# A two-layer hybrid decoder in split float32: 512-column feature blocks taken two K tiles at a time, bias rows written by GpSimd copies, and a layer norm in another order

## The chip, the cores and the metric

The kernel runs on one NeuronCore of a Trainium2 chip. The metric is the device time of one execution in microseconds (us); times before and after are medians of several runs. Beside them stands the profile of one execution, taken by the hardware profiler. Engines are named as in the profile: PE is TensorE (PEld are its weight loads), DVE is VectorE, ACT is ScalarE, POOL is GpSimd, and SP is SyncE, which issues most of the DMAs.

## The reference

Two decoder layers on 256 tokens of width 1024, all in float32. Each layer projects the stream into three head groups (retention, block-sparse attention with a relative bias, a gated convolution), joins them by an output projection, adds and normalizes; then a gated MLP of width 2816 with a causal convolution of width 3 adds and normalizes again.

```python
def reference(x, w_in, conv_w, w_out, ln1_g, ln1_b, w_up, ffn_conv_w, w_down, ln2_g, ln2_b, rel_bias):
    for l in range(DEPTH):
        mix = hybrid_mixer(x, w_in[l], conv_w[l], w_out[l], rel_bias)
        x = layer_norm(DN_ALPHA * x + mix, ln1_g[l], ln1_b[l])
        f = conv_ffn(x, w_up[l], ffn_conv_w[l], w_down[l])
        x = layer_norm(DN_ALPHA * x + f, ln2_g[l], ln2_b[l])
    return x

def conv_ffn(h, w_up, ffn_conv_w, w_down):
    u = h @ w_up
    a, b = u[..., :D_FF], u[..., D_FF:]
    a = causal_dwconv(a, ffn_conv_w)
    return (jax.nn.gelu(a.astype(F32), approximate=False) * b.astype(F32)).astype(h.dtype) @ w_down
```

In the attention, `s_own = einsum(q, k) * scale + rel_bias[t5_bucket(q_pos - k_pos)]`, with masked positions at minus infinity. With 256 tokens there is one block, so the bias of a head depends on the distance 0 to 255 alone, through 32 buckets.

## The kernel before, in words

Every float32 operand is split into a high part of reduced precision and a low rest (`split`: ACT casts, DVE subtracts), and each product is made of three: high by high, low by high, high by low. Tokens are two tiles of 128 (`NT`), the width is eight K tiles of 128 (`KD`). Weights come in units of 512 KB: SP loads a unit into `raw` (5 buffers), ACT and DVE split it into `whi` and `wlo` (6 buffers), five units ahead of PE (`LOOKAHEAD`). A scheduler sets the order of the instructions on each engine from the program, so that an edit in one place can move rows in another.

PE passes through these stages in each layer: the value projections (lines 231 to 233, `mm3`), twelve feature blocks for attention and retention (lines 318 to 320 and 407 to 409), attention and retention woven with more feature blocks, the output projection, the first norm, the MLP, the second norm. The stages that the change touches are these:

- **Wide blocks** (`wide_block`, lines 645 and 646): 30 blocks in each layer, for features 3 to 17 of the MLP. For each K tile one product of 512 columns multiplies `whi` by the high and low halves of `xx` side by side, and one of 256 columns adds `wlo` by the high half into the second half of the bank.
- **Bias rows** (`load_rows`, `load_bias`): in layer 0, after K tile 6 of the value projections, a product of the table `rel` (33 by 6) with the 0/1 matrix `bucket` (33 by 384) gives one row of 384 bias values for each head; DVE copies it from PSUM to `row`, POOL writes it to `scratch` in DRAM, and three POOL DMAs read it back into `bias`, one diagonal shift for each partition. DVE adds `bias` to the attention scores at line 456.
- **Layer norm** (`layer_norm`): for each token tile, DVE forms the sum and its statistics by halves of 512 columns, POOL raises the variance to the power of -1/2 (line 224), and DVE then subtracts and scales (line 259) and multiplies by `rstd` and adds (line 264), half by half. The halves are named h0 and h1 here. PE transposes each finished half (line 279, `turn`), ACT and DVE split the result into `xx`, and the next products read it. In the MLP's first products (`first_up`), tile 1 waits for this; four transposes of the gate values (line 609, `first_turn`) stand between.

Of the kernel before, what the change touches and what calls it, by code (L numbers as in the profile page):

```python
# [10 lines left out]
F32 = mybir.dt.float32  # L11
# [11 lines left out]
NH = 6  # L23
# [23 lines left out]
BIAS_AT = 6  # L47
# [5 lines left out]
def hybrid_decoder(ctx: ExitStack, tc: tile.TileContext, x, xw, wva, wvb, wf, wt, w_out, wg, w_up, w_down,  # L53
                   conv_w, ffn_w, ln1_g, ln1_b, ln2_g, ln2_b, rel_bias,
                   c_ident, c_rot, c_decay, c_bucket, out):
# [110 lines left out]
    rel = cp.tile([BUCKETS + 1, NH], F32, name="rel")  # L166
# [19 lines left out]
    def load_rows():  # L186

        pr = att()
        nc.tensor.matmul(pr[:NH, :HW], rel, bucket[:BUCKETS + 1, :], start=True, stop=True)
        nc.vector.tensor_copy(row[:NH, :], pr[:NH, :HW])  # L190
        nc.gpsimd.dma_start(scratch, row[:NH, :])
# [11 lines left out]
    bucket = ap.tile([P, HW], F32, name="bucket", tag="t384", bufs=6)  # L203
    row = ap.tile([P, HW], F32, name="row", tag="t384", bufs=6)
    nc.vector.memset(rel, MASKED)
    xr = x.rearrange("(t p) d -> p t d", p=P)
    spread = [lambda: load((rel[:BUCKETS, :], rel_bias), (bucket[:BUCKETS + 1, :], c_bucket)),
# [31 lines left out]
    def layer_norm(t, ps, xin, g, b, xout, store=None, after=None, between=None):  # L239
# [15 lines left out]
        done = None  # L255
        for h in range(2):
            s = slice(512 * h, 512 * h + 512)
            with behind(None if store else done):
                nc.vector.scalar_tensor_tensor(xout[:, t, s], xout[:, t, s], mv[:, 0:1], g[:, s],
                                               op0=ALU.subtract, op1=ALU.mult)  # L260
            n = 256 if store and h and t else 512
            for a in range(512 * h, 512 * h + 512, n):
                s = slice(a, a + n)
# [20 lines left out]
    for k in range(KD):  # L284
# [6 lines left out]
        if k == BIAS_AT:  # L291
            load_rows()
            for i in range(3):
                load_bias(i)
# [5 lines left out]
    for l in range(DEPTH):  # L300
# [337 lines left out]
        def wide_block(*name):  # L638
# [4 lines left out]
            for k in range(KD):  # L643
                c = slice(k * P, k * P + P)
                nc.tensor.matmul(ps, hi[:, c], xx[:, k].rearrange("p s t -> p (s t)"), start=k == 0, stop=False)  # L645
                nc.tensor.matmul(ps[:, T:], lo[:, c], xx[:, k, 0, :], start=False, stop=k == KD - 1)  # L646
# [77 lines left out]

def _constants():
# [9 lines left out]
    dist = 255 - np.arange(384)  # L735
    n = np.maximum(dist, 0)
    half = BUCKETS // 2
    large = half + (np.log(np.maximum(n, 1).astype(f) / f(half)) / f(math.log(MAX_DIST / half)) * f(half)).astype(np.int32)
    b = np.where(n < half, n, np.minimum(large, BUCKETS - 1))
    bucket = np.zeros((BUCKETS + 1, 384), f)  # L740
    for i in range(384):
        bucket[b[i] if dist[i] >= 0 else BUCKETS, i] = 1.0
# [54 lines left out]
```

## Time and profile before

| | before |
|---|---|
| median of 3 runs | 619.19 us (618.71 to 619.77) |
| the profiled execution | 619.32 us |
| its span | 617.5 us |
| granted TensorE clock | 0.996 |
| PE busy | 606.7 us, 98% |
| DVE busy | 456.1 us, 74% |
| ACT busy | 351.9 us, 57% |
| POOL busy | 15.4 us, 2% |

The span reaches from the first to the last instruction of the program; 1.8 us of the profiled execution lie around it. The duration that the profile gives to a product includes its way through the array, so that products overlap in the record. What a product costs in a row of them is read from start to start.

### The profile page before, as it was taken

How to read it: one execution, taken by the hardware profiler on the slowest of the kernel's cores; microseconds unless marked ns; L12 is line 12 of the kernel's file. 1: busy time of each engine (PE TensorE's matmuls, PEld its weight loads, DVE VectorE, ACT ScalarE, POOL GpSimd, SP SyncE). 2: the span in 40 equal slices, each digit the busy share in tenths (PEclk: the TensorE clock that was granted, in tenths of full speed). 3: DMA queues.
4: the chain of work that ended last, by engine and by line, in shares of the span. 5: the costliest groups of instructions: out<-in, count | busy, mean ns of one | idle time of the engine just before them, and what ended most of it. 6: DMA issues, size and time to landing. Idle time of an engine off the chain costs nothing.

```text
span 617.5 us, 10157 instructions
## 1 busy us (share of the span) xinstructions
PE 606.7 (98%) x3846; PEld 536.4 (87%) x3846; DVE 456.1 (74%) x834; ACT 351.9 (57%) x637; POOL 15.4 (2%) x18
## 2 busy tenths in 40 slices
PE   8999999999999999999999999999999999999994
PEld 6899998888888888899889999987888888888993
DVE  5478889787667676788765788878866767677846
ACT  6579847265555556566346795552665555656620
POOL 0100010000000000000000000101000000000001
PEclk9999999999999999999999999999999999999998
DMA  8988357465665665668428425672765666565401
GB/s 293 371 285 257 92 167 247 162 214 196 199 179 190 188 183 188 204 213 273 129 97 264 149 80 168 197 241 94 252 192 180 194 186 183 188 200 183 163 1 68
DMA packets 33676, 115.94 MB, mean 188 GB/s; under 512 B 3957, under 2 KB 4764, under 8 KB 33628
## 3 DMA queue, kind: packets, MB, share of 16 engines
q1 hardware_dynamic: 33356, 114.50, 57.6%
q0 software_dynamic: 272, 0.80, 0.4%
q8 instruction: 30, 0.49, 0.3%
q14 instruction: 18, 0.15, 0.1%
HBM read 114.22 MB, written 1.06 MB: 187 GB/s over the span
## 4 chain that ended last, share of the span: by engine, by line
PE 94%; DVE 3%; DMA 1%; POOL 1%; issue 0%; SPq 0%; ACT 0%; DVEq 0%; POOLq 0%
PE acc L645 18%; PE acc L646 9%; PE att L231 7%; PE att L232 7%; PE att L233 6%; PE acc L231 5%; PE acc L233 5%; PE acc L232 5%; PE acc L319 5%; PE acc L320 5%; PE acc L318 5%; PE acc L407 4%; PE acc L408 4%; PE acc L409 4%; PE att L346 1%; DVE x L264 1%
## 5 line engine op out<-in xcount | busy, mean ns | idle before, releaser
L83 DVE TENSOR_TENSOR wlo<-raw,whi 128x1024 fp32r<-128x1024 f32 (+3 forms) x207 | 228.5, 1115 | 80.7 <-ACT whi L82 80.2
L82 ACT CAST whi<-raw 128x1024 fp32r<-128x1024 f32 (+3 forms) x207 | 197.3, 963 | 99.0 <-PE acc L645 41.9
L645 PE MATMUL acc<-xx,whi 128*128 128x512 f32 x480 | 170.7, 398 | 0.0
L646 PE MATMUL acc<-xx,wlo 128*128 128x256 f32 x480 | 134.7, 281 | 0.0
L645 PEld LDWEIGHTS acc<-xx,whi 128*128 128x128 f32 x480 | 90.2, 188 | 22.0
L646 PEld LDWEIGHTS acc<-xx,wlo 128*128 128x128 f32 x480 | 90.6, 189 | 1.3
L319 PE MATMUL acc<-xx,whi 128*128 128x256 f32 x240 | 67.9, 283 | 0.0
L320 PE MATMUL acc<-xx,wlo 128*128 128x256 f32 x240 | 67.9, 283 | 0.0
L318 PE MATMUL acc<-xx,whi 128*128 128x256 f32 x240 | 67.9, 283 | 0.0
L407 PE MATMUL acc<-xx,whi 128*128 128x256 f32 x208 | 60.1, 289 | 0.0
L408 PE MATMUL acc<-xx,whi 128*128 128x256 f32 x208 | 58.8, 283 | 0.0
L409 PE MATMUL acc<-xx,wlo 128*128 128x256 f32 x208 | 58.8, 283 | 0.0
L232 PE MATMUL att<-whi,hl 128*128 128x512 f32 x144 | 56.5, 392 | 0.0
L233 PE MATMUL att<-wlo,hh 128*128 128x512 f32 x144 | 56.1, 389 | 0.0
L231 PE MATMUL att<-whi,hh 128*128 128x512 f32 x144 | 55.7, 393 | 0.0
L231 PE MATMUL acc<-whi,xx 128*128 128x512 f32 (+2 forms) x128 | 46.1, 363 | 1.5 <-ACT whi L82 1.3
L319 PEld LDWEIGHTS acc<-xx,whi 128*128 128x128 f32 x240 | 46.1, 192 | 0.2
L318 PEld LDWEIGHTS acc<-xx,whi 128*128 128x128 f32 x240 | 46.1, 192 | 0.2
L320 PEld LDWEIGHTS acc<-xx,wlo 128*128 128x128 f32 x240 | 46.1, 192 | 0.0
L232 PE MATMUL acc<-whi,xx 128*128 128x512 f32 (+2 forms) x128 | 44.8, 352 | 0.0
L233 PE MATMUL acc<-wlo,xx 128*128 128x512 f32 (+2 forms) x128 | 44.3, 350 | 0.0
L407 PEld LDWEIGHTS acc<-xx,whi 128*128 128x128 f32 x208 | 39.8, 191 | 0.7
(139 smaller groups left out, 938.1 us busy)
## 6 DMA issues: line engine op xcount, KB each, us to landing
raw<-in_w_up_dram SPq DMA_DIRECT2D x80, 512.0 KB, 4.4
raw<-in_w_down_dram SPq DMA_DIRECT2D x44, 512.0 KB, 4.4
raw<-in_wf_dram SPq DMA_DIRECT2D x36, 512.0 KB, 4.6
raw<-in_w_out_dram SPq DMA_DIRECT2D x16, 512.0 KB, 4.0
raw<-in_wg_dram SPq DMA_DIRECT2D x8, 512.0 KB, 4.5
raw<-in_xw_dram SPq DMA_DIRECT2D x7, 512.0 KB, 5.8
raw<-in_wt_dram SPq DMA_DIRECT2D x8, 384.0 KB, 3.2
lnp<-in_ln_g_dram SPq DMA_DIRECT2D x4, 512.0 KB, 3.8
```

What stands on the lines that cost most here:

```text
L82: nc.scalar.copy(dst_hi, src)
L83: return nc.vector.tensor_sub(dst_lo, src, dst_hi.bitcast(F32))
L231: nc.tensor.matmul(ps, lhi, rhi, start=first, stop=False)
L232: nc.tensor.matmul(ps, llo, rhi, start=False, stop=False)
L233: nc.tensor.matmul(ps, lhi, rlo, start=False, stop=last)
L318: nc.tensor.matmul(ps[:, :T], hi[:, c], xh[:, k, :], start=k == 0, stop=False)
L319: nc.tensor.matmul(ps[:, :T], hi[:, c], xl[:, k, :], start=False, stop=False)
L320: nc.tensor.matmul(ps[:, :T], lo[:, c], xh[:, k, :], start=False, stop=k == KD - 1)
L407: nc.tensor.matmul(ps[:, :T], hi[:, c], xh[:, k, :], start=k == 0, stop=False)
L408: nc.tensor.matmul(ps[:, :T], hi[:, c], xl[:, k, :], start=False, stop=False)
L645: nc.tensor.matmul(ps, hi[:, c], xx[:, k].rearrange("p s t -> p (s t)"), start=k == 0, stop=False)
L646: nc.tensor.matmul(ps[:, T:], lo[:, c], xx[:, k, 0, :], start=False, stop=k == KD - 1)
```

## The change: other orders for three pieces

Wide blocks take two K tiles at a time, the two products of 512 columns first and then the two of 256. The bias rows are written by POOL: one memset for the masked half and 32 copies of a column of `rel` (now 6 by 32) over the distances of its bucket; the matrix `bucket`, its load, the product and the DVE copy are gone. In the layer norm both halves are scaled (line 259) before either is finished (line 264).

```diff
     def load_rows():
 
-        pr = att()
-        nc.tensor.matmul(pr[:NH, :HW], rel, bucket[:BUCKETS + 1, :], start=True, stop=True)
-        nc.vector.tensor_copy(row[:NH, :], pr[:NH, :HW])
+        bound = _bucket(np.arange(T))
+        nc.gpsimd.memset(row[:NH, T:], MASKED)
+        for b in range(BUCKETS):
+            at = T - 1 - np.flatnonzero(bound == b)
+            if len(at):
+                nc.gpsimd.tensor_copy(row[:NH, at.min():at.max() + 1],
+                                      rel[:, b:b + 1].to_broadcast([NH, len(at)]))
         nc.gpsimd.dma_start(scratch, row[:NH, :])
...
-    spread = [lambda: load((rel[:BUCKETS, :], rel_bias), (bucket[:BUCKETS + 1, :], c_bucket)),
+    spread = [lambda: load((rel, rel_bias)),
...
-        done = None
         for h in range(2):
             s = slice(512 * h, 512 * h + 512)
-            with behind(None if store else done):
-                nc.vector.scalar_tensor_tensor(xout[:, t, s], xout[:, t, s], mv[:, 0:1], g[:, s],
-                                               op0=ALU.subtract, op1=ALU.mult)
-            n = 256 if store and h and t else 512
-            for a in range(512 * h, 512 * h + 512, n):
-                s = slice(a, a + n)
+            done = nc.vector.scalar_tensor_tensor(xout[:, t, s], xout[:, t, s], mv[:, 0:1], g[:, s],
+                                                  op0=ALU.subtract, op1=ALU.mult)
+        with behind(done):
+            for a, b_ in ((0, 512), (512, 768), (768, D)) if store and t else ((0, 512), (512, D)):
+                s = slice(a, b_)
                 done = nc.vector.scalar_tensor_tensor(xout[:, t, s], xout[:, t, s], rstd, b[:, s],
                                                       op0=ALU.mult, op1=ALU.add)
...
-        if k == BIAS_AT:
-            load_rows()
-            for i in range(3):
-                load_bias(i)
+    load_rows()
+    for i in range(3):
+        load_bias(i)
...
-            for k in range(KD):
-                c = slice(k * P, k * P + P)
-                nc.tensor.matmul(ps, hi[:, c], xx[:, k].rearrange("p s t -> p (s t)"), start=k == 0, stop=False)
-                nc.tensor.matmul(ps[:, T:], lo[:, c], xx[:, k, 0, :], start=False, stop=k == KD - 1)
+            for k in range(0, KD, 2):
+                for j in (k, k + 1):
+                    nc.tensor.matmul(ps, hi[:, j * P:j * P + P], xx[:, j].rearrange("p s t -> p (s t)"),
+                                     start=j == 0, stop=False)
+                for j in (k, k + 1):
+                    nc.tensor.matmul(ps[:, T:], lo[:, j * P:j * P + P], xx[:, j, 0, :],
+                                     start=False, stop=j == KD - 1)
```

On PE, inside a wide block before (line 645 is the product of 512 columns, line 646 that of 256):

```order
L645 MATMUL acc<-xx,whi 128x512
L646 MATMUL acc<-xx,wlo 128x256
L645 MATMUL acc<-xx,whi 128x512
L646 MATMUL acc<-xx,wlo 128x256
L645 MATMUL acc<-xx,whi 128x512
L646 MATMUL acc<-xx,wlo 128x256
```

The same place after (the two products stand on lines 643 and 646 there):

```order
L643 MATMUL acc<-xx,whi 128x512 x2
L646 MATMUL acc<-xx,wlo 128x256 x2
L643 MATMUL acc<-xx,whi 128x512 x2
L646 MATMUL acc<-xx,wlo 128x256 x2
L643 MATMUL acc<-xx,whi 128x512 x2
L646 MATMUL acc<-xx,wlo 128x256 x2
```

The products are the same, and the width changes after every second one instead of after every one.

On ACT, in the attention of layer 0, before: `COPY prob<-att` (line 471) brings a head's transposed probabilities back to SBUF for the value product, one copy for each of the two heads 2 and 3, and `ACTIVATE prob,sm` (line 458) is the exponential for heads 4 and 5:

```order
L82 CAST whi<-raw 128x1024
L82 CAST cath<-acc 128x256
L471 COPY prob<-att 128x384
L458 ACTIVATE prob,sm<-prob,sm 128x128
L380 COPY plain<-y 128x128
L82 CAST pair<-y 128x256
L397 COPY sw<-acc 32x256 x4
L458 ACTIVATE prob,sm<-prob,sm 128x256
L458 ACTIVATE prob,sm<-prob,sm 128x128
L458 ACTIVATE prob,sm<-prob,sm 128x256
L471 COPY prob<-att 128x384
L82 CAST whi<-raw 128x1024
```

The same place after (all lines up to two lower):

```order
L81 CAST cath<-acc 128x256
L81 CAST whi<-raw 128x1024
L469 COPY prob<-att 128x384 x2
L378 COPY plain<-y 128x128
L81 CAST pair<-y 128x256
L395 COPY sw<-acc 32x256 x4
L456 ACTIVATE prob,sm<-prob,sm 128x128
L456 ACTIVATE prob,sm<-prob,sm 128x256
L456 ACTIVATE prob,sm<-prob,sm 128x128
L456 ACTIVATE prob,sm<-prob,sm 128x256
L81 CAST whi<-raw 128x1024
```

The scheduler put the second copy beside the first, ahead of all four exponentials; nothing in the diff edits this place.

On DVE, in the first norm of tile 1, before:

```order
L252 BN_AGGR mv<-st 128x2
L223 TENSOR_SCALAR veps<-mv 128x1
L259 SCALAR_TENSOR_TENSOR x_1481<-x_1481,mv,lnp 128x512
L264 SCALAR_TENSOR_TENSOR x_1481<-x_1481,rstd,lnp 128x512
L259 SCALAR_TENSOR_TENSOR x_1481<-x_1481,mv,lnp 128x512
L264 SCALAR_TENSOR_TENSOR x_1481<-x_1481,rstd,lnp 128x512
L83 TENSOR_TENSOR xx<-att,xx 128x4x128 x2
```

The same place after:

```order
L248 BN_STATS st<-x_1508 128x6 x2
L253 BN_AGGR mv<-st 128x2
L224 TENSOR_SCALAR veps<-mv 128x1
L258 SCALAR_TENSOR_TENSOR x_1508<-x_1508,mv,lnp 128x512 x2
L263 SCALAR_TENSOR_TENSOR x_1508<-x_1508,rstd,lnp 128x512 x2
L82 TENSOR_TENSOR xx<-att,xx 128x4x128 x2
```

The second scaling stands ahead of the first finish. In the last norm, whose halves are stored to DRAM, the scheduler had this order already, and there nothing moves.

## Rows read from the trace of the kernel before

**Rows 1.** The page, chain that ended last, by engine.

```profile
PE 94%; DVE 3%; DMA 1%; POOL 1%; issue 0%; SPq 0%; ACT 0%; DVEq 0%; POOLq 0%
```

**Rows 2.** Timeline of PE, a pair of wide blocks: start, duration, line, tiles.

```profile
195.63 0.39 PE L645 MATMUL acc<-xx,whi 128*128 128x512 f32 x1
...
201.27 0.40 PE L231 MATMUL att<-whi,hh 128*128 128x512 f32 x1
```

**Rows 3.** Timeline of PE, six blocks of 256 columns: first and last product.

```profile
24.11 0.28 PE L318 MATMUL acc<-xx,whi 128*128 128x256 f32 x1
...
41.26 0.28 PE L320 MATMUL acc<-xx,wlo 128*128 128x256 f32 x1
```

**Rows 4.** Timeline of PE, a run of 512-column products: first and last.

```profile
310.71 0.39 PE L233 MATMUL acc<-wlo,xx 128*128 128x512 f32 x1
...
314.11 0.39 PE L233 MATMUL acc<-wlo,xx 128*128 128x512 f32 x1
```

**Rows 5.** Timeline of PE, value projections of layer 0: start of two runs of 512.

```profile
13.39 0.40 PE L231 MATMUL acc<-whi,xx 128*128 128x512 f32 x1
...
19.69 0.40 PE L231 MATMUL acc<-whi,xx 128*128 128x512 f32 x1
```

**Rows 6.** Timeline of PE around the product that makes the bias rows.

```profile
20.85 0.39 PE L233 MATMUL acc<-wlo,xx 128*128 128x512 f32 x1
21.16 0.81 PE L189 MATMUL att<-bucket,rel 33*6 33x384 f32 x2
...
22.12 0.28 PE L232 MATMUL acc<-whi,xx 128*128 128x256 f32 x1
```

**Rows 7.** The chain in time order, layer 0: value products of the attention (start, length).

```profile
55.82 0.80 PE acc L478 x8
...
63.95 1.34 PE acc L478 x7
```

**Rows 8.** Timeline of ACT, the copies of heads 2 and 3.

```profile
59.48 0.49 ACT L471 COPY prob<-att 128x384 f32<-128x384 f32 x1
...
63.90 0.48 ACT L471 COPY prob<-att 128x384 f32<-128x384 f32 x1
```

**Rows 9.** Timeline of DVE: the first norm of tile 1, then the stored norm.

```profile
123.56 0.74 DVE L259 SCALAR_TENSOR_TENSOR x<-x,mv,lnp 128x512 f32<-128x512 f32 x1
124.74 0.75 DVE L264 SCALAR_TENSOR_TENSOR x<-x,rstd,lnp 128x512 f32<-128x512 f32 x1 [0.43 <-POOL rstd L224]
...
604.55 1.41 DVE L259 SCALAR_TENSOR_TENSOR x<-x,mv,lnp 128x512 f32<-128x512 f32 x2
605.87 1.41 DVE L264 SCALAR_TENSOR_TENSOR x<-x,rstd,lnp 128x512 f32<-128x512 f32 x2
```

**Rows 10.** Timeline of PE, the transposes of h0 in the first norm of tile 1.

```profile
125.08 0.39 PE L233 MATMUL acc<-wlo,xx 128*128 128x512 f32 x1
125.64 0.63 PE L279 MATMUL att<-ident,x 128*128 128x128 f32 x4 [0.17 <-DVE x L264]
```

**Rows 11.** Timeline of SP and DMA issues (last column: median us to landing).

```profile
9.65 0.43 SPq L201 DMA_DIRECT2D rel<-in_rel_bias_dram  x1
rel<-in_rel_bias_dram SPq DMA_DIRECT2D x1, 0.8 KB, 4.3
bias<-scratch POOLq DMA_DIRECT2D x3, 256.0 KB, 6.6
```

**Rows 12.** Timeline of POOL.

```profile
0.28 0.10 POOL L787 MEMSET const-float32-1.0<- 128x1 f32 x1
...
22.86 0.71 POOL L191 DMA_DIRECT2D scratch<-row  x1 [22.41 <-DVE row L190]
27.86 2.17 POOL L196 DMA_DIRECT2D bias<-scratch  x3 [4.30 <-DMA scratch<-row]
116.29 0.98 POOL L224 TENSOR_TENSOR rstd<-veps,mhalf 128x1 f32<-128x1 f32 x1 [27.18 <-DVE veps L223]
```

**Rows 13.** Timeline of DVE, the first read of the bias.

```profile
42.83 0.28 DVE L456 CUSTOM_DVE_ANT_0 prob<-att,bias 128x128 f32<-128x128 f32 x1
```

More of the change, by code (lines that the diff above doesn't have):

```diff
@@ L46 @@
 WARM = 6
-BIAS_AT = 6
 WIDE = range(3, 18)
@@ L54, in hybrid_decoder @@
                    conv_w, ffn_w, ln1_g, ln1_b, ln2_g, ln2_b, rel_bias,
-                   c_ident, c_rot, c_decay, c_bucket, out):
+                   c_ident, c_rot, c_decay, out):
     nc = tc.nc
@@ L165, in hybrid_decoder @@
     xtok = xp.tile([P, NT, D], F32, name="xtok", tag="xtok", bufs=2)
-    rel = cp.tile([BUCKETS + 1, NH], F32, name="rel")
+    rel = cp.tile([NH, BUCKETS], F32, name="rel")
     ident = cp.tile([P, P], F32, name="ident")
@@ L201, in load @@
             nc.sync.dma_start(dst, src)
-    bucket = ap.tile([P, HW], F32, name="bucket", tag="t384", bufs=6)
     row = ap.tile([P, HW], F32, name="row", tag="t384", bufs=6)
-    nc.vector.memset(rel, MASKED)
     xr = x.rearrange("(t p) d -> p t d", p=P)
-    spread = [lambda: load((rel[:BUCKETS, :], rel_bias), (bucket[:BUCKETS + 1, :], c_bucket)),
+    spread = [lambda: load((rel, rel_bias)),
               lambda: load((ident, c_ident), (rot, c_rot)),
@@ L722, in hybrid_decoder, with _bucket @@
         xtok = x2
+def _bucket(dist):
+    f = np.float32
+    n = np.maximum(dist, 0)
+    half = BUCKETS // 2
+    large = half + (np.log(np.maximum(n, 1).astype(f) / f(half)) / f(math.log(MAX_DIST / half)) * f(half)).astype(np.int32)
+    return np.where(n < half, n, np.minimum(large, BUCKETS - 1))
 def _constants():
@@ L734, in _constants @@
     decay = decay * HD ** -0.5
[L735 to L742, printed above, removed]
     return {"c_ident": np.eye(P, dtype=f), "c_rot": np.ascontiguousarray(rot, dtype=f),
-            "c_decay": np.ascontiguousarray(decay, dtype=f), "c_bucket": bucket}
+            "c_decay": np.ascontiguousarray(decay, dtype=f)}
 def _lay_out(i):
@@ L776, in _lay_out @@
     }
-    for n in ("ln1_g", "ln1_b", "ln2_g", "ln2_b", "rel_bias"):
+    for n in ("ln1_g", "ln1_b", "ln2_g", "ln2_b"):
         d[n] = c(np.asarray(i[n]))
+    d["rel_bias"] = c(np.asarray(i["rel_bias"]).T)
     d.update(_constants())
```

## The prediction

> **What bounds the kernel now.** I read the chain that ended last first: PE holds 94% of it [rows 1]. So an edit is worth what it takes from PE's row of products, or what it adds to a wait of PE, and work on DVE, ACT and POOL counts only where PE waits for it. The timeline of PE, read from start to start, then gives the price of a product in each setting. Six blocks of 256 columns hold 144 products, and from the first start to the last are 143 steps in 17.15 us: 119.9 ns each [rows 3]. A run of 512 columns takes 15 steps in 3.40 us: 226.7 ns each [rows 4]. A wide block alternates the two widths; two blocks, 16 pairs, take 5.64 us, 352.5 ns a pair [rows 2]. At the prices of the two runs a pair would be 346.6 ns, so alternation costs 5.9 ns a pair. After that I looked for places where PE does something else than these steps: at the product for the bias rows, at one group of value products in layer 0, and at the first norm of tile 1.
>
> **The wide blocks.** 15 features, 2 blocks, 8 K tiles and 2 layers make 480 pairs, so all that an order of these products can give is 480 x 5.9 ns = 2.8 us. The order two and two is nowhere in the trace. The nearest row is the value projection of layer 0, which takes six products of 512 and then six of 256: three such rounds take 6.30 us, 2.10 us each [rows 5], and at the prices of the runs a round would be 6 x 346.6 ns = 2.08 us. That leaves 20 ns over 12 products, 1.7 ns a product with the width changed after every sixth, against 2.95 ns with it changed after every one. On the straight line through these two points, a change after every second product costs 1.45 + 1.5/2 = 2.2 ns a product: 8.8 ns for four products instead of 11.8. That is 3.0 ns x 240 = **0.7 us less**. Bounds: 2.8 us less, if pairs already run at the prices of the runs, and nothing, if the extra time is not one of width changes. I see no row where a run of equal widths costs more than the alternation, but a pattern that was never run can have its own price, and I keep 0.7 us more as the bound on the other side.
>
> A rule of the Trainium skill speaks against this term. By the rows, a product's step depends on what stands beside it: 346.6 ns a pair in runs, 352.5 in alternation [rows 2 to 4]. The Trainium skill, page "TensorE: Matmul & The Clock Gate", section "Back-to-back issue gap", prices an isolated step by its own columns alone, N/2.4 + 2.5 ns; by it the order of the same products would change nothing and the term would be 0. The trace's steps lie above that figure (it would be 216 and 109 ns), so the trace agrees with it only in part, and the rule stands below as a rival.
>
> The second halves of the weights are needed one step later than before, and the bank is finished by the same kind of product, so no wait changes there.
>
> **The bias rows.** PE issues a product of 512 at 20.85, then the bias product on line 189, and is at the second 256-column product after it at 22.12 [rows 6]. Without line 189 that product would start 226.7 + 119.9 ns after 20.85, at 21.20: **0.9 us less**. PE is on the chain there and its weights are split ahead of it, so I count all of it. Nothing, if PE then waits for a load, is the bound above; against it stands that DVE's copy of the rows, which made DVE's next weight split wait for PE, goes too. The load of `bucket` and a memset of DVE go as well; they are on no chain.
>
> What comes in their place is on POOL, which has nothing else to do before the norms. The table's load is issued at 9.65 and takes 4.3 us [rows 11], so the 32 copies can start at 14.0. Behind them stand on POOL's queue the write of `row` and the three reads of `bias`. From the issue of the write to that of the reads 5.0 us pass (22.86 to 27.86) [rows 12], and 6.6 us to a landing [rows 11]; with 0.3 us from the row to the issue I take 11.9 us from the last copy to the first bias. DVE reads it at 42.83 [rows 13], or 41.9 once 0.9 us are gone. So the copies may take 41.9 - 11.9 - 14.0 = 16.0 us, **0.5 us each**, before anyone waits. The trace has no POOL copy. Its nearest rows are a memset of one element per partition, 0.10 us, and a power, 0.98 us [rows 12]. A copy moves data without arithmetic, which is nearest to the memset, and all but one have 14 columns or fewer; I take 0.1 to 0.2 us, 3 to 6 us in all, hidden with 10 us to spare: **0**. The other end is a rival below.
>
> **The moved copy.** The value product of heads 2 and 3 takes 1.34 us on the chain, where the same group for heads 0 and 1 takes 0.80 [rows 7]. It waits for ACT: the copy of the first head stands at 59.48, that of the second at 63.90, just where PE is at that product [rows 8]. In the new order both copies stand together ahead of the exponentials, so the second ends some 3 us before it is needed: **0.5 us less**. The exponentials of heads 4 and 5 move back past four short copies, but the same work lies ahead of the last one, plus one copy of 0.48 us less the wait for it; PE transposes their results 2 us later. Bounds: 0.54 less, and 0 if they are late instead.
>
> **The layer norm.** DVE starts the finish of h0 1.18 us after its scaling, when POOL's power arrives (123.56, 124.74). In the stored norm, which has the new order already, the finish starts 1.32 us after the first scaling (604.55, 605.87), since two scalings need longer than POOL [rows 9]. So h0 is **0.14 us later** in six norms, and h1 earlier, by the time of one scaling. Who waits? For tile 0 PE is busy with other products, and the transposes of h0 stand in its order about when h0 is ready; I take 0.1 us for each of three norms. For tile 1 of the first norm PE waits for h0: its transposes start 0.56 us after the product ahead, where a step is 0.23 [rows 10]. There two more products now stand ahead of the transposes and fill this gap of 0.33 us, but they no longer lie behind, where they covered ACT's and DVE's split of the result, and three instead of one of the gate transposes on line 609 now stand ahead of the products that follow. So the chain from h0 over its split to `first_up` starts 0.14 us later and has less beside it; I take 0.2 us for each of two layers. In the second norm of layer 0 PE has its value products to do, and tile 1 costs nothing. Together **0.7 us more**; the bounds are 0 and, with 0.33 us more in both layers, 1.4.
>
> **The sum.** With a digit more, -0.92 - 0.54 - 0.72 + 0.70 = -1.48 on the profiled 619.32 us, 617.84. The median of the runs shown, 619.19, is 0.13 below the profiled execution, so I give **617.7** for the median after.
>
> **The rivals.** A change of 0.2%, 1.2 us, is about what a measurement of this kernel can tell from none; that puts the edges at 617.95 and 620.4.
>
> *Grouping brings the prices of the runs.* The extra 5.9 ns are then paid by the change after every product alone. For it: runs settle at 226.7 and 119.9 exactly [rows 3, 4]. Against it: the round of six and six still pays 20 ns [rows 5]. Time: 2.1 us less than the sum, 615.6.
>
> *The order of the products is worth nothing.* For it: pairs in the value projections pay too, though they change width rarely [rows 5]. Time: 0.7 us more than the sum, 618.4.
>
> *The norm's handoff costs double.* PE's wait in [rows 10] comes back whole behind the transposes instead of before them. For it: the split of h0 is the longest thing between two tiles. Against it: DVE is free earlier. Time: 0.7 us more, 618.4, and up to 619 if the copy in the attention gains nothing either.
>
> *POOL's copies are slow.* This is the one on the other side, and it decides at 0.5 us a copy. At the 0.98 us of a power [rows 12] 32 copies take 31.4 us, the first bias lands at 14.0 + 31.4 + 11.9 = 57.3, and DVE stands at line 456 from 41.9 on with the weight splits queued behind it: 15 us, 633. For it: each copy is an instruction of its own. Against it: a power is arithmetic, and a memset takes a tenth. The Trainium skill, "GPSIMD Engine Reference", section "Instruction dispatch", adds a code load of about 6 us at the first call of a freshly loaded function; no row here shows one, and by it the copies would have 10 us, 0.31 us each.
>
> **How the numbers follow.** The sum 0.45 (616.9 to 618.5), prices of the runs 0.22, order worth nothing 0.16, norm double 0.10, slow copies 0.07. Below 617.95 lie six tenths of the first and a bit more (0.29), the second and a little of the third (0.03): faster 0.54. Slower is the last rival and 0.01 of the rest: 0.08. Same 0.38. The range runs from just below the second case, 615.4, to 619.2, above the third and fourth; it leaves out the slow copies and the far ends.
>
> **What would show it.** Two wide blocks between products of 512 columns take 5.57 us or a little more (5.64 now); no product on PE between the last two K tiles of the value projections, and feature blocks 0.9 us earlier; value products of heads 2 and 3 at 0.80 us; the finish of h0 1.32 us after its first scaling; `bias` landed by 35. Wrong would be: two wide blocks at 5.64 or above, POOL copies above 0.5 us each, an idle DVE before line 454 of the new kernel, or a wait of PE behind the transposes of tile 1 that is longer than the one ahead of them was.

## The result, and the profile after

| | before | after |
|---|---|---|
| median | 619.16 us (618.71 to 619.77, 6 runs) | 615.06 us (614.53 to 615.48, 6 runs) |
| ratio | | 0.9931, 95% interval 0.9921 to 0.9941 |
| the profiled execution | 619.32 us, span 617.5 | 614.73 us, span 612.9 |

The changed kernel is 0.7% faster, 4.1 us between the medians. The forecast was 617.7 us, with a range of 615.4 to 619.2, and the time lies 0.3 us below that range. The rival "grouping brings the prices of the runs", which had 0.22, gave 615.6.

The page of the changed kernel: instructions and span, busy times, and the chain that ended last, by engine.

```profile
span 612.9 us, 10180 instructions
PE 603.8 (99%) x3844; PEld 536.2 (87%) x3844; DVE 455.0 (74%) x832; ACT 351.1 (57%) x637; POOL 23.2 (4%) x51
PE 97%; DMA 1%; DVE 1%; SPq 0%; ACT 0%; issue 0%; DVEq 0%
```

PE's share of the chain went from 94% [rows 1] to 97%. That does not measure the gain: of the three parts, run alone below, the norm has 97% at an unchanged time, and the two that bring the gain stay at 94%. Four places of the forecast can be looked up in the timelines (start, duration, engine, line). First the wide blocks on PE, a pair of them between two products of the down projection, which answers to [rows 2]:

```profile
193.29 0.61 PE L643 MATMUL acc<-xx,whi 128*128 128x512 f32 x2
193.74 0.40 PE L646 MATMUL acc<-xx,wlo 128*128 128x256 f32 x2
...
198.85 0.40 PE L232 MATMUL att<-whi,hh 128*128 128x512 f32 x1
```

The pair takes 198.85 - 193.29 = 5.56 us instead of 5.64. Next PE at the last two rounds of the value projections, where the bias product stood [rows 6]:

```profile
19.27 0.40 PE L232 MATMUL acc<-whi,xx 128*128 128x512 f32 x1
...
21.37 0.40 PE L232 MATMUL acc<-whi,xx 128*128 128x512 f32 x1
...
22.76 0.28 PE L316 MATMUL acc<-xx,whi 128*128 128x256 f32 x1
```

A full round from 512 to 512 is 2.10 us, as in [rows 5], and nothing stands between the products. Third, the chain in order of time at the value products of the attention, and ACT's copies ahead of the second group:

```profile
54.48 0.80 PE acc L476 x8
...
62.61 0.80 PE acc L476 x8
```

```profile
58.01 0.86 ACT L469 COPY prob<-att 128x384 f32<-128x384 f32 x2
```

The group of heads 2 and 3 takes 0.80 us, not 1.34 [rows 7], and both copies are over at 58.87, 3.7 us ahead of it. Last, the queue of POOL and the landing of the bias (median us), which answer to [rows 11, 12]:

```profile
13.58 7.60 POOL L192 COPY row<-rel 6x1 f32<-6x1 f32 x32 [12.66 <-DMA rel<-in_rel_bias_dram]
21.48 0.71 POOL L194 DMA_DIRECT2D scratch<-row  x1 [0.30 <-POOL row L192]
27.21 2.18 POOL L199 DMA_DIRECT2D bias<-scratch  x3 [5.02 <-DMA scratch<-row]
```

```profile
bias<-scratch POOLq DMA_DIRECT2D x3, 256.0 KB, 6.4
```

```profile
41.48 0.28 DVE L454 CUSTOM_DVE_ANT_0 prob<-att,bias 128x128 f32<-128x128 f32 x1
```

The 32 copies take 7.60 us, 0.24 us each in the mean. The bias lands about 6.4 us after its issue, near 34 us, and DVE first reads it at 41.48. So three of the four places look as forecast. The table goes through the span by the distance between the two traces at the same product, with each term beside what was forecast for it.

| stretch | forecast | between the traces | how read |
|---|---|---|---|
| value projections, from the second K tile on | -0.92 | -0.80 | 8.31 to 24.11 before, 7.76 to 22.76 after |
| attention, to the value product of heads 4 and 5 | -0.54 | -0.54 | 24.11 to 72.56, 22.76 to 70.67 |
| layer norms | +0.70 | about +0.1 | +0.05, +0.04 (first norms), +0.05 (second norm) |
| wide blocks | -0.72 | -2.70 | -1.34 in layer 0, -1.36 in layer 1 |

These four make -3.9. The traces differ by 4.6; PE also reached the second K tile 0.55 us earlier, which is most of the rest, and with this the last section deals. The two terms that miss are the norm, which costs nearly nothing, and above all the wide blocks.

### The profile page after: what moved, and what is told of

Same layout as the page of the kernel before. It is cut to its first block, busy times and chain, and to the rows that moved or that the text cites. A ratio compares the mean times of both kernels' runs of the same rounds, so it can differ in the third digit from the quotient of the medians.

```text
span 612.9 us, 10180 instructions
## 1 busy us (share of the span) xinstructions
PE 603.8 (99%) x3844; PEld 536.2 (87%) x3844; DVE 455.0 (74%) x832; ACT 351.1 (57%) x637; POOL 23.2 (4%) x51
## 4 chain that ended last, share of the span: by engine, by line
PE 97%; DMA 1%; DVE 1%; SPq 0%; ACT 0%; issue 0%; DVEq 0%
PE acc L643 18%; PE acc L646 9%; PE att L232 7%; PE att L233 7%; PE att L234 7%; PE acc L232 6%; PE acc L234 6%; PE acc L233 6%; PE acc L318 5%; PE acc L317 5%; PE acc L316 5%; PE acc L405 4%; PE acc L406 4%; PE acc L407 4%; PE att L344 1%; PE att L278 1%
## 5 line engine op out<-in xcount | busy, mean ns | idle before, releaser
L643 PE MATMUL acc<-xx,whi 128*128 128x512 f32 x480 | 150.8, 395 | 0.0
L646 PE MATMUL acc<-xx,wlo 128*128 128x256 f32 x480 | 94.6, 278 | 0.0
L643 PEld LDWEIGHTS acc<-xx,whi 128*128 128x128 f32 x480 | 75.5, 189 | 2.5
L318 PE MATMUL acc<-xx,wlo 128*128 128x256 f32 x240 | 67.9, 283 | 0.0
L407 PE MATMUL acc<-xx,wlo 128*128 128x256 f32 x208 | 58.8, 283 | 0.0
L232 PE MATMUL att<-whi,hh 128*128 128x512 f32 x144 | 55.5, 392 | 0.0
L232 PE MATMUL acc<-whi,xx 128*128 128x512 f32 (+2 forms) x128 | 46.3, 364 | 0.2
L317 PEld LDWEIGHTS acc<-xx,whi 128*128 128x128 f32 x240 | 46.1, 192 | 0.2
L316 PEld LDWEIGHTS acc<-xx,whi 128*128 128x128 f32 x240 | 46.1, 192 | 0.2
L405 PEld LDWEIGHTS acc<-xx,whi 128*128 128x128 f32 x208 | 39.8, 191 | 0.7
```

The lines of the kernel that those rows point to most:

```text
L232: nc.tensor.matmul(ps, lhi, rhi, start=first, stop=False)
L316: nc.tensor.matmul(ps[:, :T], hi[:, c], xh[:, k, :], start=k == 0, stop=False)
L317: nc.tensor.matmul(ps[:, :T], hi[:, c], xl[:, k, :], start=False, stop=False)
L318: nc.tensor.matmul(ps[:, :T], lo[:, c], xh[:, k, :], start=False, stop=k == KD - 1)
L405: nc.tensor.matmul(ps[:, :T], hi[:, c], xh[:, k, :], start=k == 0, stop=False)
L643: nc.tensor.matmul(ps, hi[:, j * P:j * P + P], xx[:, j].rearrange("p s t -> p (s t)"), start=j == 0, stop=False)
```

## The experiments

### Each part alone

Three kernels hold one part of the change each, on the kernel before: `e1_wide` the wide blocks, `e2_bias` the bias rows, `e3_norm` the norm. Expected were:

> The kernel before with the new order in the wide blocks alone. Theory A, that the extra time of an alternation grows by a straight line with how often the width changes (the step of the prediction): 0.7 us less than before, two wide blocks in 5.59 us. Theory B, that pairs already run at the prices of the runs: 2.7 to 2.8 us less, two wide blocks in 5.55 us. Theory C, that the order is worth nothing: no difference, 5.64 us.

> The kernel before with the bias rows by GpSimd copies alone; the scheduler's order of the two copies on ScalarE comes with it. If each part acts for itself as its row was read: 0.9 us less for the product that is gone and 0.5 us less for the moved copy, 1.4 to 1.5 us less in all, with the value products of heads 2 and 3 at 0.80 us on the chain. If the first feature block came earlier in the changed kernel for another reason than the product (it came 1.35 us earlier in its trace), up to 1.9 us less.

> The kernel before with the new order in the layer norm alone. By the prediction's step: 0.7 us more. By the trace of the changed kernel, where the distance to the kernel before moves by 0.1 us over all three norms: no difference that can be told, 0.0 to 0.2 us more.

| | median us | ratio to before, 95% interval |
|---|---|---|
| wide blocks | 616.57 | 0.9954 (0.9941 to 0.9968) |
| bias rows | 617.73 | 0.9975 (0.9966 to 0.9985) |
| layer norm | 619.06 | 0.9997 (0.9988 to 1.0005) |

Against the 619.14 of the kernel before in these comparisons that is -2.57, -1.41 and -0.08; the sum, -4.06, is the whole of the 4.10 as far as these times can tell, so the parts do not touch each other. The bias rows bring what the forecast had for them, -0.92 - 0.54 = -1.46, and the moved copy belongs to them: it is in this kernel and not in the other two. The norm costs nothing measurable instead of 0.7, and the wide blocks bring close to the 2.8 of the rival, not 0.7.

Why the norm is free is to be seen in the changed kernel, on DVE and then on PE, in the first norm of tile 1 (to be read against [rows 9, 10]):

```profile
121.81 1.41 DVE L258 SCALAR_TENSOR_TENSOR x<-x,mv,lnp 128x512 f32<-128x512 f32 x2
123.13 1.41 DVE L263 SCALAR_TENSOR_TENSOR x<-x,rstd,lnp 128x512 f32<-128x512 f32 x2
```

```profile
123.78 0.39 PE L233 MATMUL acc<-whi,xx 128*128 128x512 f32 x1
124.02 0.63 PE L278 MATMUL att<-ident,x 128*128 128x128 f32 x4
124.41 0.48 PE L234 MATMUL acc<-wlo,xx 128*128 128x512 f32 x1
124.72 0.60 PE L278 MATMUL att<-ident,x 128*128 128x128 f32 x4
125.33 0.51 PE L232 MATMUL acc<-whi,xx 128*128 128x512 f32 x1
125.82 0.55 PE L607 MATMUL acc<-ident,gsb 128*128 128x128 f32 x3
```

The finish of h0 starts 1.32 us after the first scaling, as forecast. The products ahead now fill the gap before the transposes, 0.24 us from product to transposes where it was 0.56. Behind the transposes of h1 the rows open by about as much as this gap closed: 0.61 us for four transposes, then 0.49 us for one product. In the kernel with the norm alone, whose distance to before was -0.32 us at the first product of the output projection (108.41 against 108.73), the transposes of h0 come 0.26 us later (125.58 against 125.64), but the last gate transpose only 0.05 us (134.94 against 135.21). So tile 1's later turn is paid back. The likely reason, which no run separates, is that h1 is ready sooner: its transposes start 0.70 us behind those of h0, not 1.64 (125.64 and 127.28 before). The forecast named h1's earlier finish and counted only the lost cover behind the transposes. In layer 1 the same three places read -0.27, -0.01 and -0.24, so 0.03 us is left there.

### What is it in the order of the widths?

One product of each kind per K tile (before) and two (after) differ in two ways: the width changes less often, and a 256-column product no longer directly follows the 512-column product that reads the same K tile of `xx` and writes the same half bank. Four kernels are the changed kernel with another order of the same products in a wide block.

```diff
 # e5_lag: 512 and 256 in turn, but the 256 belongs to the K tile before
+for k in range(KD):
+    high(k)
+    if k:
+        low(k - 1)
+low(KD - 1)
 # e6_four and e7_eight
-            for k in range(0, KD, 2):
-                for j in (k, k + 1):
+            for k in range(0, KD, 4):
+                for j in range(k, k + 4):
 # e8_bank: 512 and 256 in turn, the 256s in a bank of their own
+ps2 = acc()
-nc.tensor.matmul(ps[:, T:], lo[:, c], xx[:, k, 0, :], start=False, stop=k == KD - 1)
+nc.tensor.matmul(ps2[:, :T], lo[:, c], xx[:, k, 0, :], start=k == 0, stop=k == KD - 1)
+nc.vector.tensor_add(y, ps2[:, :T], y)
```

(`high(k)` and `low(k)` stand for the products of 512 and 256 columns of K tile k; in `e7_eight` all 4s are 8s.)

> The changed kernel with the widths alternating again inside a wide block, but the product of 256 columns one K tile behind the one of 512, so that it never reads the half of the stream that the product just ahead of it read. If the extra time comes from the sequence of widths: 2.2 to 2.7 us more than the changed kernel, pairs at 352 to 353 ns. If it comes from reading the same K tile twice in a row: no difference to the changed kernel, pairs at 347 ns.

> The changed kernel with four K tiles at a time, four products of 512 columns and then four of 256. If groups of two already run at the prices of the runs: within 0.3 us of the changed kernel. If each change of width costs something of its own: up to 0.7 us less.

> The changed kernel with all eight products of 512 columns of a wide block first and then all eight of 256. If groups of two already run at the prices of the runs: within 0.3 us of the changed kernel. If what a group pays is what the groups of six in the value projections pay (20 ns in a round of 12): 30 blocks in each layer, each one round, 1.2 us more.

> The changed kernel with the widths alternating again, and the products of 256 columns in a bank of PSUM of their own (one VectorE addition more for each block). If the extra time comes from two products in turn on the same half of a bank: pairs at 347 ns on TensorE. If it comes from the sequence of widths: pairs at 352 to 353 ns, 2.7 us more than the changed kernel or a little above, by the addition.

Two more orders came later: groups of three, three and two K tiles (`e9_three`), and pairs shifted by one product, 512, then 256 256 512 512 and so on (`e13_shift`).

> The changed kernel with its wide blocks in groups of three, three and two K tiles instead of two, two, two and two; nothing else differs. Measured so far for two wide blocks after a stretch of equal widths: one K tile at a time 5.64 us, two 5.56, four 5.59, eight 5.56. Theory 'the price follows the length of the runs' (short runs pay at each change, long runs at few): three lies between two and four, two wide blocks 5.56 to 5.59 us, 0 to 1.0 us more than the changed kernel's 615.06. Theory 'two is a lucky pattern': the steps after a change depend on what ran several products before, and only some sequences close cheaply; then three can lie outside this interval, as high as the alternation, 5.64 us and 2.5 us more.

> The changed kernel with the pairs shifted by one product: 512, then 256 256 512 512 and so on, and 256 512 256 at the end; the same 16 products in a block, with nine changes of width instead of seven (alternation has 15). From one line-232 product to the same product twelve features later the traces read 99.52 us by two, 100.64 alternating, 99.76 by three, 100.24 by four, 99.67 by eight. Theory 'short runs of two are cheap': the shifted pairs keep it but for the end of the block, 99.5 to 99.8 us, 0 to 0.7 us more than the changed kernel's 615.06. Theory 'what counts is where a run stands, not its length': the first 256 comes after a single 512, and the steps can be as dear as by four or in alternation, 100.2 to 100.6, 1.8 to 2.8 us more.

PE does nothing but its products in this stage, so one distance tells the price without the noise of the start: from the first down product of a feature of layer 0 to that of the twelfth feature after it, with 24 wide blocks and 144 products of 512 columns between. At the prices of the runs, 346.6 ns a pair and 226.7 ns a product [rows 3, 4], it would be 24 x 8 x 346.6 + 144 x 226.7 ns = 99.19 us. The distance also holds what the blocks do to the down products behind them. PE in the changed kernel, then with four K tiles at a time:

```profile
165.68 0.40 PE L232 MATMUL att<-whi,hh 128*128 128x512 f32 x1
...
265.20 0.40 PE L232 MATMUL att<-whi,hh 128*128 128x512 f32 x1
```

```profile
166.31 0.40 PE L232 MATMUL att<-whi,hh 128*128 128x512 f32 x1
...
266.55 0.40 PE L232 MATMUL att<-whi,hh 128*128 128x512 f32 x1
```

That is 99.52 and 100.24 us. In layer 1 every kernel's distance is the same as in layer 0 to 0.01 us. The last columns set what all 30 features make of it (2.5 times the difference to 99.52) beside the medians.

| order in a block | changes of width | 12 features, us | above the run prices, ns a pair | 30 features, us over after | median, us over after |
|---|---|---|---|---|---|
| before, in turn | 15 | 100.64 | 7.6 | +2.8 | |
| `e8_bank`, in turn | 15 | 100.64 | 7.6 | +2.8 | +3.0 |
| `e5_lag`, in turn, shifted operand | 13 | 100.32 | 5.9 | +2.0 | +1.9 |
| `e13_shift`, twos, shifted | 9 | 99.92 | 3.8 | +1.0 | +1.2 |
| after, by two | 7 | 99.52 | 1.7 | 0 | 0 |
| `e9_three` | 5 | 99.76 | 3.0 | +0.6 | +0.7 |
| `e6_four` | 3 | 100.24 | 5.5 | +1.8 | +1.8 |
| `e7_eight` | 1 | 99.68 | 2.6 | +0.4 | +1.0 |

Two answers are firm. The bank is not the cause: with the 256s in a bank of their own the distance is the same 100.64 as before. Nor is it the shared operand: `e5_lag` parts the two products of a K tile and keeps most of the price. The weight tile changes with the width too (`whi` for 512, `wlo` for 256), but the feature blocks of [rows 3] also change it, at one width, and step by 119.9 ns. What is left is the sequence of the widths. A third answer went against both expectations of `e6_four`: the price does not fall steadily with fewer changes. By two it is lowest, by four two thirds of what by two saves are lost, by eight it is low again. By three it lies between two and four, and the shifted pairs lie between the ranges of their two theories. (In the trace of `e7_eight` some 0.5 us more is another thing: a single late stretch in layer 0, between 265 and 276 us, beyond this distance.)

The ns starts of the trace show how it comes about. Each order settles into a fixed pattern that repeats to 1 ns; the first block behind down products starts from their 227 and then falls into it. The steps, in ns. In turn: 236, 113, 232, 118, 241, 120. By two: 233, 236, 116, 113, 232, 231, 113, 119. By four: 233, 236, 228, 232, 118, 119, 118, 117, 235, 233, 236, 224, 117, 120, 120, 120. By eight, after the 256s: 233, 236, 228, 233, 231, then 227 for the rest, and 113, 119, then 120. The first 256 behind settled 512s takes 113 ns, 7 less than its run price, and by eight the 512s behind the 256s take 6, 9, 1, 6 and 4 ns more than 227 before they settle. By two, three of every four 256s are 4 to 7 ns short, which pays back most of that. By four, seven of eight 512s are long and the 256s only up to 3 ns short. So the length of a run is not the whole of it. What makes a step of 228 or 236 after the same neighbour stays open; in turn, by two, by four and by eight each weight load starts 2 to 5 ns after the product ahead of its own, so the trace shows no late load to put it on. `e13_shift` fits this: where its pairs stand as by two the steps are the same, and its extra sits behind the single products at the ends of the blocks and at the start of the next.

The order that the change chose is the best of the seven that ran.

### How much room the bias has

`e4_copies3` makes each POOL copy three times, in the changed kernel.

```diff
-                nc.gpsimd.tensor_copy(row[:NH, at.min():at.max() + 1], rel[:, b:b + 1].to_broadcast([NH, len(at)]))
+                for _ in range(3):
+                    nc.gpsimd.tensor_copy(row[:NH, at.min():at.max() + 1], rel[:, b:b + 1].to_broadcast([NH, len(at)]))
```

> The changed kernel with each of the 32 GpSimd copies issued three times, which changes no value. At the 0.24 us that a copy took, 96 copies end 15.2 us later, at 36.4 us. If the slack of the prediction is right (11.9 us from the last copy to the first bias, a read at 41.4 us): the first bias lands at about 48.5 us and 5 to 7.5 us are added to the changed kernel. If the copies cost through contention with VectorE's subtractions instead, the subtractions of the first 40 us get longer than 0.96 and 1.23 us, and time is added ahead of the first read. If there is more slack than I worked out: nothing is added.

Measured: 616.5 us, ratio to before 0.9958 (0.9944 to 0.9971), 1.4 us over the changed kernel. POOL, DVE, and the list of what PE waited for between 40 and 58 us:

```profile
13.61 20.19 POOL L193 COPY row<-rel 6x1 f32<-6x1 f32 x96 [12.69 <-DMA rel<-in_rel_bias_dram]
37.78 2.18 POOL L200 DMA_DIRECT2D bias<-scratch  x3 [2.96 <-DMA scratch<-row]
```

```profile
43.45 0.29 DVE L455 CUSTOM_DVE_ANT_0 prob<-att,bias 128x128 f32<-128x128 f32 x1 [1.45 <-DMA bias<-scratch]
```

```profile
PE att L469 <- DVE prob L462: 1.3, 1, 1.3
```

The wait came where it was forecast, DVE at the first read of the bias and PE behind it, and nowhere else: the rest of the span keeps its distance of 1.9 us to the changed kernel (0.43 of it from the start). It is smaller than expected, since the write of `row` landed in 3.0 us, not 5.0, and the 96 copies took 0.21 us each. The copies had 20.19 - 1.45 = 18.7 us of room, 0.58 us a copy; with the 5.0 us of the changed kernel's write it would be 16.7 us, 0.52 a copy, as an estimate. The forecast's point of decision was 0.5, and the copies need 0.24.

That 0.24 is a mean of two things. POOL in the changed kernel, ten copies and then one, and DVE beside the one:

```profile
17.27 1.25 POOL L192 COPY row<-rel 6x1 f32<-6x1 f32 x10
18.59 1.20 POOL L192 COPY row<-rel 6x4 f32<-6x4 f32 x1
```

```profile
18.52 1.23 DVE L82 TENSOR_TENSOR wlo<-raw,whi 128x1024 fp32r<-128x1024 f32 x1 [1.23 <-ACT whi L81]
```

While DVE stands idle ten copies take 1.25 us, 0.12 us each from start to start. A copy that starts during one of DVE's subtractions ends only behind it, in these traces without exception: all six copies over 0.3 us (0.38 to 1.20) end 0.04 us after a subtraction does, and in `e4_copies3` all ten do within 0.05. The subtractions keep their 0.96 and 1.23 us. So the contention of the second theory is there, but POOL pays for it and not DVE.

### More blocks in the wide form

The last four features of each layer take three products of 256 columns for each K tile, 360 ns against about 348 for a wide pair. `e10_late` makes them wide (`WIDE = range(3, 22)`), `e11_all` the six query and key blocks of each layer as well.

> The changed kernel with the last four features of each layer as wide blocks too (they take three products of 256 columns for each K tile, 120 ns each, 360 ns; grouped by two a wide pair took 347.7 ns in the changed kernel). 4 features x 2 blocks x 8 K tiles x 2 layers = 128 K tiles x 12.3 ns = 1.6 us less than the changed kernel, 613.5 us, if PE is all that counts. Rival: each of these blocks gets one more copy on ACT and one more addition on DVE (0.4 us each) in the stretch ahead of the norm, and if PE waits there for a feature or a weight split the gain is eaten: 614.5 to 616.

> The same, and the six query and key blocks of each layer as wide blocks too: 2 x 6 x 8 = 96 K tiles more, 1.2 us less than with the late features alone, 612.3 us, if PE is all that counts. Rival: in layer 0 the first of these blocks stand at the start of the attention, where the bias rows are read and DVE and ACT split the weights just ahead of PE; six more copies and additions of 0.4 us each there delay the first scores and PE waits for them: no gain over the late features alone or up to 2 us lost.

Measured: 616.59 us (ratio 0.9957, 0.9943 to 0.9971) and 617.03 us (0.9968, 0.9956 to 0.9981), both slower than the changed kernel. In `e10_late` the blocks themselves came out as expected, 0.77 us less in layer 0 and 0.75 in layer 1, but layer 0 lost about 2 us at its last feature and in its second norm. (The two traces differ by 1.7 us; the other 1.0 lies ahead of these blocks, at the start, with which the last section deals.) Busy times by stretch (start and end, length, then PE, PEld, DVE, ACT and POOL with their counts, clock, DMA share, GB/s) of the changed kernel and then of `e10_late`, and PE in `e10_late` at the loss:

```profile
278.00:294.00 16.00, 16.00 (x135) 15.96 (x134) 13.58 (x20) 9.67 (x16) 0.00 (x0) 1.00 0.79 262
```

```profile
278.00:294.00 16.00, 16.00 (x94) 13.96 (x93) 15.26 (x24) 12.13 (x21) 0.00 (x0) 1.00 0.79 258
```

```profile
299.03 0.39 PE L232 MATMUL att<-hhi,hh 128*128 128x512 f32 x1
300.13 0.74 PE L232 MATMUL att<-hhi,hh 128*128 128x512 f32 x2 [0.72 <-ACT hh L81]
...
306.33 1.32 PE L278 MATMUL att<-ident,x 128*128 128x128 f32 x8
307.66 0.62 PE L232 MATMUL acc<-whi,xx 128*128 128x512 f32 x2
308.38 0.50 PE L233 MATMUL acc<-whi,xx 128*128 128x512 f32 x1
```

Each wide block adds a copy on ACT and an addition on DVE. DVE, which splits the next layer's value weights there, goes from 13.6 to 15.3 of 16 us, the last feature is late, and PE waits for its `hh`: 1.10 us from 299.03 to the next start, where a step is 0.23, so 0.9 of the 2. Most of the rest is lost at the norm, whose eight transposes now stand in a row with no down product between them; in the changed kernel they stand in two groups of four, at 303.41 and 305.30, with six products between. That the busy DVE makes the feature late is read from these rows, and no run shows it alone. In `e11_all` PE waits 0.9 us at the last feature of layer 0 and 0.8 us at that of layer 1 (1.7 together in its list of waits, `att L232 <- ACT hh`), and 0.8 us at score products near 73 us; at the first scores, where the rival had it, it does not wait. Layer 1 has no such weights to split, so two more kernels took the late features wide in layer 1 alone: all four (`e12_second`), and the first three of them (`e14_three_late`).

```diff
-            if f in WIDE:
+            if f in WIDE or (l == DEPTH - 1 and f > 2):              # e12_second
+            if f in WIDE or (l == DEPTH - 1 and 2 < f < NF - 1):     # e14_three_late
```

> The changed kernel with the last four features as wide blocks in the second layer alone. Theory 'in the first layer the late wide blocks lose it': with them in both layers the stretch before the late products of the down projection got 0.77 us shorter in each layer, but in the first layer VectorE was busy for 15.3 of the 16 us from 278 on (it splits the value weights of the next layer there), the last feature came late and PE lost 2.0 us; in the second layer it was busy 17.4 of 25 us and PE lost nothing. So 64 K tiles x 12.3 ns = 0.8 us less than the changed kernel: 614.3 us, the stretch to the end of the second layer 0.75 us shorter, no wait of PE there. Rival: the loss has another place, and the time stays at 615.1 or above.

> The changed kernel with features 18, 19 and 20 of the second layer as wide blocks too, and the last feature as it was: with the last one wide as well, the stretch ahead was 0.74 us shorter, and PE then waited 0.74 us for that feature, whose copy on ACT and addition on DVE stand right ahead of its last split. If that is the whole loss, 3 features x 2 blocks x 8 K tiles x 12.3 ns = 0.6 us less than the changed kernel, 614.5 us, and no wait of PE at the end of the down projection. Rival: the feature before it is late instead, and nothing is gained: 615.1.

`e12_second`: 615.1 us (ratio 0.9924, 0.991 to 0.9938), no gain over the changed kernel's 615.06. PE at the end of its down projection:

```profile
594.58 0.39 PE L234 MATMUL att<-hlo,hh 128*128 128x512 f32 x1
595.17 0.50 PE L232 MATMUL att<-hhi,hh 128*128 128x512 f32 x1 [0.20 <-ACT hh L81]
595.63 0.50 PE L233 MATMUL att<-hhi,hl 128*128 128x512 f32 x1
595.97 0.40 PE L234 MATMUL att<-hlo,hh 128*128 128x512 f32 x1
```

The 0.74 us that the blocks gained are lost in three steps of 0.59, 0.46 and 0.34 where a product takes 0.23, at the last feature, whose copy and addition stand right ahead of its last split.

That is not the whole of it, since `e10_late` has the same four features wide in layer 1 and no wait there. ACT at the split of the last but one down weight, in `e10_late` and then in `e12_second`:

```profile
577.01 1.05 ACT L81 CAST hhi<-raw 128x1024 fp32r<-128x1024 f32 x1 [1.40 <-DMA raw<-in_w_down_dram]
```

```profile
577.08 1.05 ACT L81 CAST hhi<-raw 128x1024 fp32r<-128x1024 f32 x1 [2.41 <-DMA raw<-in_w_down_dram]
```

The load of this weight was issued at 573.64 and at 572.70, so it took 3.4 us in the one and 4.4 in the other (4.4 in the changed kernel too). PE stands 0.8 us earlier in `e12_second`, but ACT and DVE, whose work for the features is queued behind this split, do not. So the feature comes 0.3 us after PE wants it, where in `e10_late` it was 0.4 us ahead: the late features wide leave so little room that the landing of one load decides.

With the last feature left as it was, `e14_three_late` has no such wait, its trace is 0.57 us shorter there, and it takes 614.48 us (614.01 to 614.65; ratio to before 0.9926, 0.9913 to 0.994). That is the lowest median of all kernels here, 0.6 us under the changed kernel, as expected. By the ratios, each taken beside its own runs of the kernel before, it is 0.3 us, and `e12_second` comes out at 0.4. The intervals overlap, so the step in the trace shows the gain of `e14_three_late` and the times do not separate either kernel from the changed one.

## Why the prediction was wrong

**The wide blocks: the mechanism was right, the size was not.** The step that failed is the "straight line through these two points", alternation and the round of six and six, which put 8.8 ns on four products and 0.7 us on the term. The runs give 100.64 - 99.52 = 1.12 us for 192 pairs, 5.8 ns a pair, 2.8 us for 480, and -2.70 and -2.57 when read from the traces and the time of the part alone. The line had a flaw that could be seen without a run: at no change at all it keeps 1.45 ns a product, while [rows 3, 4] are runs with no change, by which the extra is nothing by definition. Through that third point the three do not lie on a line. The experiments then contradict any such line, also a better one: fewer changes made it dearer by three and four. The working has a second slip: "two wide blocks ... 5.57 us" among the signs does not follow from its own term, which gives 16 x 351.0 ns = 5.62; 5.56 was measured.

**The rival that came nearest.** "Grouping brings the prices of the runs" had the size right, 2.8 us, and that is in part luck. Over twelve features the alternation lies 7.6 ns a pair above the prices of the runs, not 5.9: [rows 2] ends with the blocks, and the first five down products behind them take 232, 236, 228, 233 and 230 ns where the run settles at 227. And pairs by two do not reach the prices of the runs, they pay 1.7 ns. The gain is the difference, 5.8, which happens to be near the 5.9 of the rival. What spoke against it, the 20 ns of a round of six and six, was a good reading: the order by eight still pays for one change what six and six does. It was wrong to take that as a lower bound for shorter groups.

**The order does count.** The Trainium skill, page "TensorE: Matmul & The Clock Gate", section "Back-to-back issue gap", prices an isolated step by its columns alone, 216 and 109 ns here. These steps are not isolated, and the runs show two things that such a price leaves out: the same products in another order cost 2.6 us more or less, and a 512-column step took 224 to 241 ns, depending on what stood up to five products before it.

**The layer norm.** The term "0.7 us more" measured about 0.1 in the traces and nothing in the time of the part alone. Its first half was right: h0 is 0.14 us later. The failed step is the 0.2 us for the lost cover behind the transposes of tile 1 in each of two layers, and 0.1 us for each tile 0: in the trace PE turns h1 0.7 us behind h0, sooner than before, and what waits moves without growing.

**The bias product** (-0.92), **the moved copy** (-0.54) and **the copies on POOL** (0, with 0.5 us a copy as the point of decision) held. The kernel with this part alone gained 1.41 of 1.46, and its value projections, from the second K tile on, went from 15.80 us to 14.87 (8.29 to 23.16); a copy alone took 0.12 us, within the 0.1 to 0.2 assumed, but the waits for DVE's subtractions, which the forecast did not have, made it 0.24, and the room was 0.58 where it was measured. The Trainium skill, "GPSIMD Engine Reference", section "Instruction dispatch", has a code load of about 6 us at a first call; no such time lies among these copies, nor does the first start later than its load, for which the row has POOL waiting up to 13.58; one that was over within this wait no run here shows or excludes.

**The sum.** With the terms as measured alone, -2.57 - 1.41 - 0.08 = -4.06; with the forecast's, -1.48. The difference of 2.6 is 1.9 us of the wide blocks and 0.8 of the norm, less 0.05 of the bias rows.

## What to carry to other kernels

When the price of an order that was never run is put between two that were, add the point of no change at all; if the three do not lie on a line, no line through two of them sizes the fourth, and both bounds stay open. Where products of two widths alternate on PE, an order by two and two is worth a test, and so is the group's length: here by two gave 5.8 ns a pair and by four a third of that. A form that is cheaper on PE pays only where the engines that finish it (here a copy on ACT and an addition on DVE for each block) have room, and least of all right ahead of a handoff, where the landing of one load can decide whether PE waits.

## What the runs showed of the hardware that was not expected

The step of a product on PE depends on several products before it, up to five in the order by eight, with fixed patterns that repeat to 1 ns and a price that does not fall steadily with the length of the runs (the table above).

A copy on POOL that meets one of DVE's subtractions waits for its end: the 16 copies over 0.3 us in the two traces above all end 0.04 to 0.05 us after a subtraction does, and the subtractions are no longer for it.

The start of the span differs between the profiled executions, of which there is one for each kernel, by more than the smallest effects here. PE reached its first feature block between 22.76 and 24.38 us in those of the kernels that have the new bias rows. One cause is the length of the first steps. PE in the changed kernel, then in `e10_late`, at the start:

```profile
6.48 0.53 PE L232 MATMUL acc<-whi,xx 128*128 128x512 f32 x1
6.84 0.40 PE L234 MATMUL acc<-wlo,xx 128*128 128x512 f32 x1
7.08 0.40 PE L233 MATMUL acc<-whi,xx 128*128 128x512 f32 x1
```

```profile
7.33 0.63 PE L234 MATMUL acc<-wlo,xx 128*128 128x512 f32 x1
7.76 0.63 PE L233 MATMUL acc<-whi,xx 128*128 128x512 f32 x1
8.19 0.63 PE L234 MATMUL acc<-wlo,xx 128*128 128x512 f32 x1
```

In `e10_late` a 512-column product still takes 0.43 us from start to start at 8.19, in the changed kernel 0.24 us from 6.84 on, although the granted clock from 6 to 10 us reads 1.00, the level of 2.4 GHz, in both. The other cause is the load of the second K tile: the second K tile's first product starts at 7.76 in the changed kernel and at 8.31 before. That execution had the shortest start of all. So 0.55 us of the 4.6 between the two profiles is put down to chance; the medians, 4.1 us apart, do not have it. No second profile of a kernel shows this, but `e12_second` speaks for it: its profiled execution, with the longest start, took 616.32 us, and its four others 615.00 to 615.11.
